# A two-layer trunk kernel: state-space channels projected first, rotation angles computed directly, array halves in turn

## The chip, the cores and the metric

One core of one Trainium2 chip runs the whole program. The metric is the device time of one execution in microseconds, taken as the median over executions of the same program; the profile is of one more execution.

## The reference

One inference step of a trunk of two layers for two request groups that share the weights. Cut to what matters here, layer 0:

```python
z = rmsnorm(x, g_mix[0]) @ w_in_mix        # columns: u (512) | q (512) | k (128) | v (128)
ya = s5_mixer(u, ...)                      # 32 groups of 16 channels, 64 complex states each:
                                           #   h_t = a h_{t-1} + b u_t,  y = Re(c h),  a = exp((lr + i li) dt)
yb = swa(q, k, v, rel_bias, sink)          # window of 128, 8 query heads on 2 key-value heads of 64
x = x + concat([ya, yb]) @ w_out_mix
x = x + conv_ffn(rmsnorm(x, g_ffn[0]))     # up-projection, causal convolution of width 3, gelu gate, down-projection
...
```

Layer 1 replaces the mixer by a convolution module and is not touched. Prompts have 1040 tokens (16 learned ones and 1024); 8 decoding requests add 8 tokens each with cached keys, values and states. Everything is float32 at the interface.

## The kernel before

The tokens are split into two streams that stay in SBUF with channels on partitions: **A** has 528 prompt tokens, **B** the other 512 prompt tokens and the 64 decoding ones (576). Every weight block goes through one path: DMA of a raw float32 tile, a rounded high part `whi` on ScalarE (L210), a low part `wlo` on VectorE (L216), and then for every 128 rows of the contraction three products with the high and low parts of the activations (L315), each over two halves of the stream's tokens. These are the `pu` rows of the trace: 264 columns for A, 288 for B, two matmuls each.

`run(items)` goes through a list of `Unit`s (one weight block on one stream; a `Pair` is two with one activation). After each of a Unit's contraction steps it calls `pump()`, which advances a list of background generators at their rates. The generators emit the work that isn't a projection: transposing the inputs (`take_x`, from L506), the tables of the state-space part (`s5_prep`, L823 to L879), its main loop (`s5_main`, L923 to L971), the attention of the prompts. An instruction's place in its engine's queue is the moment of emission, so the list of Units and the generators' `yield`s set the order on every engine; nothing is reordered afterwards. When the list asks for a result that a generator hasn't emitted, it pumps without Units until it has (`back()` waits so for the four parts of A's attention output, `atp`).

**Input projections.** `in_units` lists a stream's four u blocks, k, v and four q blocks. Before, A goes k and v as a Pair, q, then u; B goes u, then k, v, q. The epilogue of a u block is one VectorE operation of eight pieces (`us`, L1397), that of q and k one of 128x528 (`qst`, L530). `NU0` is how many u blocks must have been projected before `s5_main` starts; `nq`, counted by q's epilogue, releases A's attention.

**State-space part.** `s5_prep1` computes a = decay·(cos, sin) on VectorE and ScalarE. `s5_rot` makes the powers of the rotation by repeated squaring in small GpSimd operations (L709 to L726), combines them into tables ta and tb, and multiplies these into the four tables tj of 128x576 (L588 to L596) which go to DRAM. `table_e` and `table_f` build the tables ee (L823 to L828) and ff (L843 to L848) on VectorE, which PE transposes (psk L865, psf L879). `s5_main` runs eight iterations over four groups: stage 1 (L923) forms the chunk sums xr and xi, writing each half of the columns of the array; stage 2 scans on VectorE; stage 3 (L968 to L970) accumulates, for each half g2 and each gl, one product of 128 rows and two of 64 rows, twelve matmuls of 138 columns, in one PSUM bank per half.

**Prompt attention.** `attn_blocks` runs over tasks: for A one of 16 queries, one with 144 keys and three with 256 keys; for B four with 256 keys. A task is split by key-value head into two half-tasks of four query heads. A half-task computes scores (sps L1236, four matmuls of 64 rows in two emissions), adds the bias on VectorE (L1239), takes maxima (L1171), exponentials on ScalarE (L1178), normalizes (L1187), transposes the probabilities (tps L1218, evacuated by ScalarE L1220) and multiplies by v (ops L1256, 64 columns). Three half-tasks are in flight, with two buffers each for P, PT and q. A's attention runs at rate 1.6 beside the projections, B's at 0.7 beside the first up-projection of A.

## Time and profile before

| what | value |
|---|---|
| median of 3 runs | 2460.75 us (2455.71 to 2464.07) |
| profiled execution | 2459.83 us, of it 2457.7 us span |
| PE busy | 2386.9 us (97% of the span) |
| VectorE busy | 1695.9 us (69%) |
| ScalarE busy | 1001.6 us (41%) |
| GpSimd busy | 237.0 us (10%) |
| mean granted TensorE clock | 0.98 |
| chain that ended last | PE 86%, VectorE 6%, ScalarE 2%, DMA 1% |

The span runs from the first to the last instruction; the 2.1 us by which the execution is longer lie outside it. The chain goes back from the last instruction, at each step to what released it: four fifths of it are the projections of L315. A granted clock of 1.00 is the upper of TensorE's two levels, 2.4 GHz; a mean below that holds stretches at 1.2 GHz.

### The profile page before, as it was taken

The page shows a single profiled execution, that of the slowest core. Times are in us where ns is not written, and L with a number is a line of the kernel's source. Part 1 is how long each engine was busy: PE and PEld are TensorE (multiplying, and loading weights), DVE is VectorE, ACT ScalarE, POOL GpSimd, SP SyncE. Part 2 cuts the span into 40 slices and gives each one's busy share as a digit, 9 for nine tenths or more (in the row PEclk, how much of TensorE's full clock was granted, in tenths as well). Part 3 has the DMA queues.
Part 4 walks back from the last instruction along what each step waited for, and adds up shares of the span by engine and source line. Part 5 has one row for each costly group of instructions (what it writes and reads, how often), then busy time and mean ns, then how long its engine had stood idle before and what let it go on. Part 6 is the DMA issues. An engine that isn't in the chain of part 4 may idle for free.

```text
span 2457.7 us, 46157 instructions
## 1 busy us (share of the span) xinstructions
PE 2386.9 (97%) x18180; PEld 2313.4 (94%) x18180; DVE 1695.9 (69%) x3180; ACT 1001.6 (41%) x1912; POOL 237.0 (10%) x557
## 2 busy tenths in 40 slices
PE   7689999999999999999999999999999999999998
PEld 6677889888999999999999999999999999999998
DVE  6976657554477679888888567888889765444343
ACT  6133354664334343342426443443434534333333
POOL 5940120000000000110101000100000000000000
PEclk9889999999999999999999999999999999999999
DMA  7765753423333433222232432333232423222222
GB/s 211 222 128 134 223 147 118 111 68 95 97 93 89 137 100 97 82 82 85 80 89 70 129 125 74 101 92 95 86 98 80 130 74 114 80 87 79 86 85 70
DMA packets 459598, 260.86 MB, mean 106 GB/s; under 512 B 57451, under 2 KB 446727, under 8 KB 458198
## 3 DMA queue, kind: packets, MB, share of 16 engines
q1 hardware_dynamic: 456246, 253.08, 35.5%
q0 software_dynamic: 3136, 4.85, 0.8%
q8 instruction: 143, 2.34, 0.4%
q14 instruction: 73, 0.60, 0.1%
HBM read 225.59 MB, written 35.52 MB: 106 GB/s over the span
## 4 chain that ended last, share of the span: by engine, by line
PE 86%; DVE 6%; ACT 2%; DMA 1%; issue 1%; SPq 0%; POOL 0%; DVEq 0%; ACTq 0%
PE pu L315 80%; DVE wlo L216 1%; PE ops L1256 1%; PE sps L1236 1%; PE yps L969 1%; PE tps L1218 0%; PE yps L968 0%; ACT whi L210 0%; PE psum_s L367 0%; DMA xbD<-xB 0%; PE yps L970 0%; DMA e<-eD 0%; DVE xA L1187 0%; DVE mx L1171 0%; DVE us L1397 0%
## 5 line engine op out<-in xcount | busy, mean ns | idle before, releaser
L216 DVE TENSOR_TENSOR wlo<-raw,whi 128x512 fp32r<-128x512 f32 x720 | 489.8, 683 | 529.1 <-ACT whi L210 520.2
L210 ACT CAST whi<-raw 128x512 fp32r<-128x512 f32 x720 | 434.9, 608 | 695.1 <-PE pu L315 641.8
L1658 DVE SCALAR_TENSOR_TENSOR xA<-gl,pt,xA 128x528 f32<-128x528 f32 x240 | 183.2, 764 | 3.8 <-ACT xA L1652 1.5
L1658 DVE SCALAR_TENSOR_TENSOR xB<-gl,pt,xB 128x512 f32<-128x512 f32 x240 | 179.3, 747 | 4.3 <-ACT xB L1652 2.9
L1477 ACT ACTIVATE cv<-cv 128x592 f32<-128x592 f32 (+2 forms) x88 | 58.9, 670 | 154.5 <-DVE cv L1476 154.5
L1475 DVE SCALAR_TENSOR_TENSOR cv<-G,pt,cv 128x592 f32<-128x592 f32 (+2 forms) x88 | 70.1, 796 | 40.7 <-ACT cv L1474 40.0
L315 PE MATMUL pu<-a0h,whi 128*128 128x288 f32 (+3 forms) x428 | 91.5, 296 | 5.1 <-ACT a0h L212 1.9
L315 PE MATMUL pu<-a1h,whi 128*128 128x288 f32 (+3 forms) x428 | 92.0, 297 | 0.0
L315 PE MATMUL pu<-a4h,whi 128*128 128x288 f32 (+3 forms) x420 | 89.1, 294 | 2.6 <-ACT th L1405 2.5
L315 PE MATMUL pu<-a3h,whi 128*128 128x288 f32 (+3 forms) x428 | 91.1, 294 | 0.0
L315 PE MATMUL pu<-a2h,whi 128*128 128x288 f32 (+3 forms) x428 | 90.5, 293 | 0.0
L315 PE MATMUL pu<-a0l,whi 128*128 128x288 f32 (+3 forms) x428 | 90.1, 292 | 0.3 <-DVE a0l L218 0.3
L315 PE MATMUL pu<-a1h,wlo 128*128 128x288 f32 (+3 forms) x428 | 90.1, 293 | 0.0
L315 PE MATMUL pu<-a1l,whi 128*128 128x288 f32 (+3 forms) x428 | 90.0, 292 | 0.0
L315 PE MATMUL pu<-a0h,wlo 128*128 128x288 f32 (+3 forms) x428 | 89.8, 292 | 0.0
L315 PE MATMUL pu<-a7h,whi 128*128 128x288 f32 (+3 forms) x420 | 89.4, 295 | 0.0
L315 PE MATMUL pu<-a3h,wlo 128*128 128x288 f32 (+3 forms) x428 | 89.3, 290 | 0.0
L315 PE MATMUL pu<-a5h,whi 128*128 128x288 f32 (+3 forms) x420 | 89.1, 294 | 0.0
L315 PE MATMUL pu<-a2l,whi 128*128 128x288 f32 (+3 forms) x428 | 89.1, 290 | 0.0
L315 PE MATMUL pu<-a3l,whi 128*128 128x288 f32 (+3 forms) x428 | 89.0, 290 | 0.0
L315 PE MATMUL pu<-a6h,whi 128*128 128x288 f32 (+3 forms) x420 | 89.0, 294 | 0.0
L315 PE MATMUL pu<-a6l,whi 128*128 128x288 f32 (+3 forms) x420 | 88.0, 291 | 0.7 <-DVE a6l L216 0.7
(665 smaller groups left out, 6943.1 us busy)
## 6 DMA issues: line engine op xcount, KB each, us to landing
raw<-in_ffn_w_up SPq DMA_DIRECT2D x352, 256.0 KB, 2.9
raw<-in_ffn_w_down SPq DMA_DIRECT2D x128, 256.0 KB, 2.8
raw<-in_conv_w_pw SPq DMA_DIRECT2D x96, 256.0 KB, 2.8
raw<-in_ffn_w_down SPq DMA_DIRECT2D x64, 192.0 KB, 2.5
xbD<-xB SPq DMA_DIRECT2D x3, 2304.0 KB
xB<-xbD SPq DMA_DIRECT2D x6, 1152.0 KB
raw<-in_w_in_mix SPq DMA_DIRECT2D x24, 256.0 KB, 3.8
xaD<-xA SPq DMA_DIRECT2D x2, 2112.0 KB
```

The lines of the kernel that those rows point to most:

```text
L210: nc.scalar.copy(hi, src)
L216: nc.vector.tensor_tensor(lo, src, hi.bitcast(F32), op=OP.subtract)
L315: nc.tensor.matmul(ps[:, ch, :c], wt, xt[:, off + ch * c:off + (ch + 1) * c], start=(k == 0 and pi == 0), stop=(k == nk - 1 and pi == 2))
L969: nc.tensor.matmul(out, E[hs, 0, gl, :], H[hs, 0, gl, :], start=False, stop=False)
L1236: nc.tensor.matmul(v[:, hh, :], q[hs, 2 * pr + hh, :], self.kT[hs, kc0:kc0 + nk], start=True, stop=True)
L1256: nc.tensor.matmul(v, vt[:m, hs], d["PT"][k], start=(k == 0), stop=(k == len(vsegs) - 1))
L1475: nc.vector.scalar_tensor_tensor(c, G[:, 1:1 + n], wc(1), c, op0=OP.mult, op1=OP.add)
L1477: self.chain(lambda: None, lambda: None, lambda: nc.scalar.activation(c, c, AF.Gelu_apprx_tanh))
L1658: V.scalar_tensor_tensor(acc, gl[:, i:i + npp], w(i), acc, op0=OP.mult, op1=OP.add)
```

## The change

Five things are edited, all in layer 0's mixer.

1. The order of the input projections is now u of A, u of B, then k, v, q of A, then k, v, q of B; `NU0` falls from 8 to 6, and `nq` counts A's q blocks alone.
2. `s5_rot` computes the angles of ta and tb directly: the angle times a multiple, reduced by 2π in three parts, in fourteen GpSimd operations per table (16x16 and 16x9 columns), with the absolute value on VectorE and two sines on ScalarE. The tables tj come in halves with buffers of their own. The count of GpSimd's rows falls from 495 to 347.
3. Stage 3 takes both halves at once in two PSUM banks: four products of 128 rows, then eight of 64 rows that alternate between the upper and the lower half of the array's rows.
4. `attn_blocks` takes all eight heads as one task: scores alternate between the two halves of the rows (one per key-value head), outputs between the two halves of the columns, with one copy for both. P has one buffer, PT two; w1 and w2 are counts of `yield`s that spread a task.
5. `take_x` copies the second half of each of B's tiles on VectorE and not on ScalarE.

```diff
-NU0 = 8
+NU0 = 6
...
+                (nc.vector.tensor_copy if first or hf else nc.scalar.copy)(
                     x[:, 4 * hf:4 * hf + 4, lo:hi], f[:, :, lo - off:hi - off])
...
+        thh, thl = pl[:, 16, :], pl[:, 17, :]
+        V.tensor_scalar(thh, th, 12288.0, -12288.0, op0=OP.add, op1=OP.add)
+        V.tensor_tensor(thl, th, thh, op=OP.subtract)
...
     def s5_rot(self):
...
-        G.tensor_copy(e[:, 0, 0, :], cs)
-        G.tensor_copy(e[:, 0, 1, :], sn)
-        renorm(e[:, 0, 0, :], e[:, 0, 1, :])
-        for _ in range(3):
-            square(e[:, 0, 0, :], e[:, 0, 1, :], e[:, 0, 0, :], e[:, 0, 1, :])
-        for i in range(1, 8):
-            square(e[:, i, 0, :], e[:, i, 1, :], e[:, i - 1, 0, :], e[:, i - 1, 1, :])
...
+        for tt, mult in ((ta, self.mult[:, 0:16]), (tb, self.mult[:, 16:25])):
+            n = tt.shape[3]
+            v = lambda i: tz[:, 256 * i:256 * i + 16 * n].rearrange("p (g a) -> p g a", g=16)
+            x, k, w, h = (v(i) for i in range(4))
+            mb = mult.unsqueeze(1).to_broadcast([P, 16, n])
+            th = lambda i: self.pl[:, i, :].unsqueeze(2).to_broadcast([P, 16, n])
+            G.tensor_tensor(k, th(4), mb, op=OP.mult)
+            G.tensor_scalar(k, k, 1.0 / (2 * math.pi), MAGIC, op0=OP.mult, op1=OP.add)
+            G.tensor_scalar(k, k, MAGIC, None, op0=OP.subtract)
+            G.tensor_tensor(x, th(16), mb, op=OP.mult)
+            for c in TWOPI[:2]:
+                G.tensor_scalar(h, k, -c, None, op0=OP.mult)
+                G.tensor_tensor(x, x, h, op=OP.add)
+            G.tensor_tensor(w, th(17), mb, op=OP.mult)
+            G.tensor_scalar(h, k, -TWOPI[2], None, op0=OP.mult)
+            G.tensor_tensor(w, w, h, op=OP.add)
+            G.tensor_tensor(x, x, w, op=OP.add)
+            G.tensor_scalar(x, x, 3.1415925, -3.1415925, op0=OP.min, op1=OP.max)
+            nc.vector.scalar_tensor_tensor(h, x, -1.0, x, op0=OP.mult, op1=OP.max)
+            G.tensor_scalar(h, h, -1.0, math.pi / 2, op0=OP.mult, op1=OP.add)
+            nc.scalar.activation(tt[:, 0], h, AF.Sin)
+            nc.scalar.activation(tt[:, 1], x, AF.Sin)
         for j in range(4):
             g4 = slice(4 * j, 4 * j + 4)
-            tt = pp.tile([P, 2, 4, 9, 16], F32, name="tj", tag="tj")
             t1 = tz[:, 0:576].rearrange("p (g q b) -> p g q b", g=4, q=9)
             t2 = tz[:, 576:1152].rearrange("p (g q b) -> p g q b", g=4, q=9)
             f1 = lambda ri: ta[:, ri, g4, :].unsqueeze(2).to_broadcast([P, 4, 9, 16])
             f2 = lambda ri: tb[:, ri, g4, :].unsqueeze(3).to_broadcast([P, 4, 9, 16])
-            self.cmul(G, tt[:, 0], tt[:, 1], f1(0), f1(1), f2(0), f2(1), t1, t2)
             for ri in range(2):
-                nc.gpsimd.dma_start(self.dq(self.tD, ri, j, 132),
-                                    tt[:, ri].rearrange("p g q b -> p g (q b)")[:, :, 0:132])
+                G.tensor_tensor(t1, f1(0), f2(ri), op=OP.mult)
+                G.tensor_tensor(t2, f1(1), f2(1 - ri), op=OP.mult)
+                tt = pp.tile([P, 4, 9, 16], F32, name="tj", tag=f"tj{ri}")
+                G.tensor_tensor(tt, t1, t2, op=OP.add if ri else OP.subtract)
+                G.dma_start(self.dq(self.tD, ri, j, 132), tt.rearrange("p g q b -> p g (q b)")[:, :, 0:132])
...
-        def stage3(i, g2, ys):
+        def stage3(i, ys):
+
             u, m1, E, H = u_(i), m_(i), e_(i), h_(i)
-            ps = self.bank("yps")
-            hs = slice(64 * g2, 64 * g2 + 64)
+            mm = lambda out, w, x, start, stop: nc.tensor.matmul(out, w, x, start=start, stop=stop,
+                                                                 skip_group_check=True)
+            pss = [self.bank("yps"), self.bank("yps")]
+            out = lambda g2, gl: pss[g2][:, gl * NK:(gl + 1) * NK]
+            for g2 in range(2):
+                for gl in range(2):
+                    mm(out(g2, gl), m1[:, 2 * gl + g2, :], u[:, 2 * gl + g2, :], gl == 0, False)
             for gl in range(2):
-                out = ps[:, gl * NK:(gl + 1) * NK]
-                nc.tensor.matmul(out, m1[:, 2 * gl + g2, :], u[:, 2 * gl + g2, :], start=True, stop=False)
-                nc.tensor.matmul(out, E[hs, 0, gl, :], H[hs, 0, gl, :], start=False, stop=False)
-                nc.tensor.matmul(out, E[hs, 1, gl, :], H[hs, 1, gl, :], start=False, stop=True)
-            nc.scalar.copy(ys.rearrange("p (l h) k -> p l h k", h=2)[:, :, g2, :],
-                           ps[:, :2 * NK].rearrange("p (g k) -> p g k", g=2))
-            if g2:
-                for g in range(4):
-                    nc.gpsimd.dma_start(dap(self.yD, (4 * i + g) * 16 * 8 * NK, [[NK, 8], [8 * NK, 16], [1, NK]]),
-                                        ys[:, g, :])
+                for ri in range(2):
+                    for g2 in range(2):
+                        hs = slice(64 * g2, 64 * g2 + 64)
+                        mm(out(g2, gl), E[hs, ri, gl, :], H[hs, ri, gl, :], False, ri == 1)
+            for g2 in range(2):
+                nc.scalar.copy(ys.rearrange("p (l h) k -> p l h k", h=2)[:, :, g2, :],
+                               pss[g2][:, :2 * NK].rearrange("p (g k) -> p g k", g=2))
+            for g in range(4):
+                nc.gpsimd.dma_start(dap(self.yD, (4 * i + g) * 16 * 8 * NK, [[NK, 8], [8 * NK, 16], [1, NK]]),
+                                    ys[:, g, :])
...
-        self.atA = SB[:, 2048:2048 + 4 * 528].rearrange("p (j n) -> p j n", j=4)
-        v4 = lambda c, k: SA[:, c:c + 4 * k].rearrange("p (h k) -> p h k", h=4)
-        self.abuf = {"P": [v4(0, 256), v4(1024, 256)], "PT": [v4(2048, P), v4(2560, P)],
-                     "q": [v4(3072, P), v4(3584, P)]}
+        self.atA = SA[:, 2048:2048 + 4 * 528].rearrange("p (j n) -> p j n", j=4)
+        v8 = lambda t, c, k: t[:, c:c + 8 * k].rearrange("p (h k) -> p h k", h=8)
+        self.abuf = {"P": [v8(SA, 0, 256)], "PT": [v8(SB, 2048, P), v8(SB, 3072, P)],
+                     "q": [SB[:, 4096:4608].rearrange("p (h k) -> p h k", h=4)]}
...
         self.nbuf[kind] = self.nbuf.get(kind, 0) + 1
-        return self.abuf[kind][self.nbuf[kind] % 2]
...
-            self.nq += 1
+            self.nq += s is self.A
...
+        def turn(pt, task):
+            nq, out = task[1], []
+            for k, (vt, ko, m) in enumerate(task[5]):
+                t = self.buf("PT")[:m, :, :nq]
+                for kv in range(2):
+                    v = self.bank("tps").rearrange("p (h k) -> p h k", h=4)[:m, :, :nq]
+                    for h in range(4):
+                        nc.tensor.transpose(v[:, h, :], pt[:, 4 * kv + h, ko:ko + m], self.ident[:nq, :nq])
+                    nc.scalar.copy(t[:, 4 * kv:4 * kv + 4], v)
+                out.append(t)
+                yield out
+
+        def scores(i):
+            c0, nq, kc0, nk, bcol = tasks[i][:5]
+            q = qs[i]
+            pt = self.abuf["P"][0][:nq, :, :nk]
+            for pr in range(2):
+                vs = [self.bank("sps").rearrange("p (h k) -> p h k", h=2)[:nq, :, :nk] for _ in range(2)]
+                for hh in range(2):
+                    for kv, hs in enumerate(half):
+                        nc.tensor.matmul(vs[kv][:, hh, :], q[hs, 2 * pr + hh, :], self.kT[hs, kc0:kc0 + nk],
+                                         start=True, stop=True)
+                for kv in range(2):
+                    h0 = 4 * kv + 2 * pr
+                    V.scalar_tensor_tensor(pt[:, h0:h0 + 2, :], vs[kv], HD ** -0.5,
+                                           self.bias[:nq, h0:h0 + 2, bcol:bcol + nk], op0=OP.mult, op1=OP.add)
+                if pr == 0:
+                    yield pt
+
+        def output(task, pts):
+            c0, nq, kc0, nk, bcol, vsegs, oc = task
+            v = self.bank("ops").rearrange("p (h k) -> p h k", h=4)[:, :, :nq]
+            for k, (vt, ko, m) in enumerate(vsegs):
+                for kv, hs in enumerate(half):
+                    nc.tensor.matmul(v[hs], vt[:m, hs], pts[k][:, 4 * kv:4 * kv + 4, :],
+                                     start=(k == 0), stop=(k == len(vsegs) - 1))
+            nc.scalar.copy(at[:, :, oc:oc + nq], v)
...
+        n = len(tasks)
+        live = None
+        for i in range(n + 1):
+            if live:
+                pt, sm, es = live
+                self.softmax_fin(pt, 8, sm, es)
+                for _ in range(w2):
                     yield
-            if 0 <= i - 1 < n:
-                d = live[i - 1]
-                self.softmax_fin(d["P"], 4, *d["s"])
+                for pts in turn(pt, tasks[i - 1]):
+                    yield
+            if i < n:
+                for pt in scores(i):
+                    yield
+                live = (pt, *self.softmax_rows(pt, tasks[i][1], 8, tasks[i][3], self.sink, self.nsink))
+                load_q(i + 1)
+                yield
+            if i:
+                output(tasks[i - 1], pts)
                 yield
...
+                for _ in range(w1):
+                    yield
...
-        yield from self.attn_blocks(tasks, at)
+        yield from self.attn_blocks(tasks, at, 6, 3)
...
-        yield from self.attn_blocks(tasks, at)
+        yield from self.attn_blocks(tasks, at, 3, 2)
...
-        def in_units(s, h):
-            us = [Unit(self.wblock(win, 0, KT, j * P), h, s, self.epi_u(s, j)) for j in range(4)]
-            ks = [Unit(self.wblock(win, 0, KT, 1024), h, s, self.epi_k(s)),
-                  Unit(self.wblock(win, 0, KT, 1152), h, s, self.epi_v(s))]
-            return us, ks + [Unit(self.wblock_q(j), h, s, self.epi_q(s, j)) for j in range(4)]
-        uA, kA = in_units(A, lambda: self.hx["A"])
-        uB, kB = in_units(B, lambda: self.hx["B"])
-        items += [Pair(kA[0], kA[1])] + kA[2:] + uA + uB + kB
+        hA, hB = (lambda: self.hx["A"]), (lambda: self.hx["B"])
+        us = [[Unit(self.wblock(win, 0, KT, j * P), h, s, self.epi_u(s, j)) for j in range(4)]
+              for s, h in ((A, hA), (B, hB))]
+        items += [Pair(us[0][0], us[0][1])] + us[0][2:] + us[1]
+        for s, h in ((A, hA), (B, hB)):
+            items += [Unit(self.wblock(win, 0, KT, 1024), h, s, self.epi_k(s)),
+                      Unit(self.wblock(win, 0, KT, 1152), h, s, self.epi_v(s))]
+            items += [Unit(self.wblock_q(j), h, s, self.epi_q(s, j)) for j in range(4)]
```

The tail of A's prompt attention in PE's order (`sps` scores, `tps` transposes, `ops` outputs, `pu` projections; the last `pu` row ahead of the tail is the end of the input projections). Before:

```order
L1236 MATMUL sps<-kT,xA 128x256 x2
L315 MATMUL pu<-y5h,whi 128x288 x2
L315 MATMUL pu<-y5l,whi 128x288 x2
L315 MATMUL pu<-y5h,wlo 128x288 x2
L1256 MATMUL ops<-xA,vA 64x512 x2
L315 MATMUL pu<-y6h,whi 128x288 x2
L315 MATMUL pu<-y6l,whi 128x288 x2
L315 MATMUL pu<-y6h,wlo 128x288 x2
L1218 MATMUL tps<-ident,xA 128x128 x4
L315 MATMUL pu<-y7h,whi 128x288 x2
L315 MATMUL pu<-y7l,whi 128x288 x2
L315 MATMUL pu<-y7h,wlo 128x288 x2
```

and with the change:

```order
L321 MATMUL pu<-y7h,whi 128x288 x2
L321 MATMUL pu<-y7l,whi 128x288 x2
L321 MATMUL pu<-y7h,wlo 128x288 x2
L1232 MATMUL ops<-xB,vm 64x512 x2
L1232 MATMUL ops<-xB,vA 64x512 x2
L1205 MATMUL tps<-ident,xA 128x128 x16
L1218 MATMUL sps<-kT,xB 128x256 x8
L1232 MATMUL ops<-xB,vA 64x512 x4
L1205 MATMUL tps<-ident,xA 128x128 x16
L1218 MATMUL sps<-kT,xB 128x256 x8
L1232 MATMUL ops<-xB,vA 64x512 x4
L1205 MATMUL tps<-ident,xA 128x128 x16
L1232 MATMUL ops<-xB,vA 64x512 x4
```

Before, each emission of attention has three or more rows of projection behind it until the attention's end; now the last three tasks stand behind the last input projection with no projection between them.

The start on ScalarE, from the sine of the base angle (table load and `pl`), over the copies of the rope table (`Rk`), to the input transposes of B (squares into `junk`, copies of `xps`). Before:

```order
L673 ACT_TABLE_LOAD
L673 ACTIVATE pl<-pl 128x16
L674 ACTIVATE pl<-pl 128x16
L390 COPY Rk<-rps 128x512
L391 COPY Rk<-rps 128x16
L496 ACTIVATE junk,ssqB<-xrow 128x512
L508 COPY xB<-xps 128x4x128
L496 ACTIVATE junk,ssqB<-xrow 128x512
L508 COPY xB<-xps 128x4x128
```

and with the change:

```order
L678 ACT_TABLE_LOAD
L678 ACTIVATE pl<-pl 128x16
L679 ACTIVATE pl<-pl 128x16
L396 COPY Rk<-rps 128x512
L397 COPY Rk<-rps 128x16
L731 ACTIVATE ta<-tz 128x256
L732 ACTIVATE ta<-tz 128x256
L731 ACTIVATE tb<-tz 128x144
L732 ACTIVATE tb<-tz 128x144
L502 ACTIVATE junk,ssqB<-xrow 128x512
L514 COPY xB<-xps 128x4x128
```

Four sines of tables that GpSimd computes now stand ahead of the squares and copies of stream B.

## Rows read from the trace of the kernel before

**Rows 1.** Busy time by window: start:end, length; then each engine, clock, DMA share, GB/s.
```profile
30.00:122.00 92.00, 64.83 (x489) 59.44 (x488) 80.44 (x173) 36.35 (x87) 83.47 (x188) 0.87 0.72 218
122.00:389.00 267.00, 254.10 (x1681) 217.05 (x1679) 179.69 (x425) 108.11 (x273) 57.29 (x74) 0.94 0.58 152
440.00:600.00 160.00, 159.07 (x1140) 136.73 (x1139) 86.37 (x171) 91.49 (x190) 3.33 (x20) 1.00 0.28 81
```

**Rows 2.** PE's waits, 0 to 150 us: total us, times, longest.
```profile
PE psf L879 <- DVE ff L845: 10.9, 3, 5.0
PE vps L1159 <- ACT xB L508: 6.6, 1, 6.6
```

**Rows 3.** Timeline, GpSimd then ScalarE: start us, duration us; [idle before <-releaser].
```profile
30.51 0.19 POOL L725 COPY e<-pl 128x16 f32<-128x16 f32 x1 [21.31 <-ACT pl L674]
...
110.03 1.17 POOL L588 TENSOR_TENSOR tz<-ta,tb 128x576 f32<-128x576 f32 x1
111.16 1.94 POOL L589 TENSOR_TENSOR tz<-ta,tb 128x576 f32<-128x576 f32 x1
...
47.81 0.62 ACT L210 CAST whi<-raw 128x512 fp32r<-128x512 f32 x1 [5.78 <-DMA raw<-in_w_in_mix]
```

**Rows 4.** Timeline, VectorE, table work without and with GpSimd beside it.
```profile
71.19 1.04 DVE L843 TENSOR_TENSOR ff<-bb,apw 128x512 f32<-128x512 f32 x1
...
97.09 0.70 DVE L530 TENSOR_TENSOR qst<-pu,Rk 128x528 f32<-128x528 f32 x1
...
109.28 1.55 DVE L1397 TENSOR_TENSOR us<-pu,Rk 128x66 f32<-128x66 f32 x8
...
111.99 1.98 DVE L844 TENSOR_TENSOR y<-bb,apw 128x512 f32<-128x512 f32 x1
...
119.68 1.78 DVE L848 TENSOR_TENSOR ff<-ff,y 128x512 f32<-128x512 f32 x1
```

**Rows 5.** Timeline, PE, one state-space iteration: stage 1, then part of stage 3.
```profile
210.52 0.69 PE L923 MATMUL xr<-u,xf 128*64 128x138 f32 x8
211.04 0.64 PE L923 MATMUL xi<-u,xf 128*64 128x138 f32 x8
...
250.97 0.40 PE L968 MATMUL yps<-u,m 128*128 128x138 f32 x2
...
255.25 0.53 PE L315 MATMUL pu<-y1h,whi 128*128 128x288 f32 x2
```

**Rows 6.** Timeline, PE, prompt attention of A between projection rows.
```profile
176.74 1.13 PE L1236 MATMUL sps<-kT,xA 64*128 64x256 f32 x4
177.80 0.53 PE L315 MATMUL pu<-y3h,whi 128*128 128x288 f32 x2
178.17 0.42 PE L315 MATMUL pu<-y3l,whi 128*128 128x288 f32 x2
178.44 0.42 PE L315 MATMUL pu<-y3h,wlo 128*128 128x288 f32 x2
...
181.62 1.93 PE L1256 MATMUL ops<-xA,vA 128*64 128x512 f32 x4
183.48 0.53 PE L315 MATMUL pu<-y6h,whi 128*128 128x288 f32 x2
```

**Rows 7.** Groups of VectorE, then ScalarE, 440 to 600 us: busy us, mean ns.
```profile
L1239 DVE SCALAR_TENSOR_TENSOR P<-sps,bias 128x512 f32<-128x512 f32 x16 | 10.9, 686 | 2.8 <-PE sps L1236 2.8
L1171 DVE TENSOR_REDUCE mx<-P 128x4 f32<-128x1024 f32 x8 | 9.8, 1220 | 0.3
L1187 DVE TENSOR_SCALAR P<-P,smx 128x256 f32<-128x256 f32 x32 | 9.2, 350 | 0.3
...
L1178 ACT ACTIVATE P<-P,nm 128x256 f32<-128x256 f32 x32 | 15.9, 496 | 11.0 <-DVE nm L1173 10.8
L1220 ACT COPY PT<-tps 128x512 f32<-128x512 f32 x16 | 9.3, 585 | 5.7 <-PE tps L1218 5.3
L1178 ACT ACTIVATION_READ_ACCUMULATOR P<-P,nm 128x1 f32 x34 | 6.3, 187 | 0.0
```

**Rows 8.** Timeline, PE, first norm sums of stream A after the mixer.
```profile
388.61 1.17 PE L367 MATMUL psum_s<-ones,acc 128*128 128x1 f32 x10
```

More of the change, by code (lines that the diff above doesn't have):

```diff
@@ L60 @@
 Q2 = 5
+MAGIC = 12582912.0
+_C2 = math.floor((2 * math.pi - 6.28125) * 2 ** 21) / 2 ** 21
+TWOPI = (6.28125, _C2, 2 * math.pi - 6.28125 - _C2)
 class Stream:
@@ L98, with __init__ @@
 class Unit:
-    def __init__(self, w, act, s, epi, off=0, c=None):
+    def __init__(self, w, act, s, epi, off=0, c=None, hold=False):
         self.w = w
+        self.hold = hold
         self.act = act
@@ L316, in mm @@
                                          start=(k == 0 and pi == 0), stop=(k == nk - 1 and pi == 2))
-            for u in units if len(units) == 1 else ():
+            for u in units if len(units) == 1 and not units[0].hold else ():
                 for i, (k0, n) in enumerate(u.w.cuts):
@@ L507, in take_x @@
                 squares(2 * t + hf)
-                (nc.vector.tensor_copy if first else nc.scalar.copy)(
+                (nc.vector.tensor_copy if first or hf else nc.scalar.copy)(
                     x[:, 4 * hf:4 * hf + 4, lo:hi], f[:, :, lo - off:hi - off])
@@ L1187, in softmax_fin, with attn_blocks @@
             V.tensor_scalar(pt[:, h, :], pt[:, h, :], sm[:, h:h + 1], None, op0=OP.mult)
-    def attn_blocks(self, tasks, at):
+    def attn_blocks(self, tasks, at, w1, w2):
         nc = self.nc
         V = nc.vector
-        todo = [(t, kv) for t in tasks for kv in range(2)]
-        qs, live = {}, {}
+        qs = {}
+        half = [slice(0, 64), slice(64, 128)]
         def load_q(i):
```

119 lines of the change are left out of this document (19 added, 100 removed).

## The prediction

> **What bounds the kernel now.** I read the table of windows first [rows 1]. Between 30 and 122 us PE works 64.83 of 92 us while VectorE works 80.44 and GpSimd 83.47; the granted clock is 0.87 there. Between 122 and 389 us PE works 254.10 of 267 us at 0.94, and between 440 and 600 us, beside B's attention, 159.07 of 160 us at 1.00. So there are three regimes. In the first PE waits for others, and a shorter PE instruction is worth nothing. In the last a PE microsecond saved is a microsecond of the total. The second lies between: 12.9 us of idle time. The list of PE's waits [rows 2] says what it waits for at the start: 10.9 us for the table ff of VectorE, and once 6.6 us for ScalarE's copies of stream B. The first regime ends when ff's last operation ends on VectorE, at 119.68 + 1.78 = 121.46 us [rows 4]; the second at the first norm sums of A, 388.61 us [rows 8]. I price the change as a shift of these two points and of the stage behind.
>
> **First regime: the start, +23 us.** GpSimd gets its angle at 30.51 us [rows 3], as now. The sines of the first table need 13 of its operations of 256 columns, one absolute value on VectorE and one more operation; the second table the same at 144 columns. No row has these sizes. A 16-column operation lasts 0.19 us, a 576-column one 1.17 us [rows 3]; between them in proportion, 256 columns cost 0.6 us and 144 columns 0.4 us, together 14 x 0.6 + 14 x 0.4 = 14 us, and with the handovers and four sines ScalarE is past them near 47 us. Between ends far apart (28 operations at 0.19 give 36 us, at 1.17 give 63 us) I take the middle because the sizes lie there. ScalarE's queue holds the squares and copies of B behind the sines, 16.5 us late. VectorE has taken over some copies and gives perhaps 1.5 us back. The weight casts behind them waited 5.78 us for a DMA before, until 47.81 us [rows 3], and that wait absorbs the next 5 us: +10. PE's 6.6 us wait on these copies is inside, and grows.
>
> The u blocks of A now come first, so four epilogues of 1.55 us stand on VectorE where 0.70 us ones stood [rows 4]: +3.5.
>
> Then contention. Operations on table ff last 1.04 us with GpSimd on small operations, 1.98 us beside its 576-column ones [rows 4], which themselves go from 1.17 to 1.94 us [rows 3]. All 24 such GpSimd operations and their DMAs now start near 47 us and run some 40 us beside the tables; before only six ran there. If VectorE spends three quarters of 40 us on operations that lose 0.94 of every 1.98 us, that is 14 us, less the 5 us that the last table already paid: +9. The sum is +23. The ends: +6 with the sines past at 36 us and half the contention, +40 with them past at 63 us.
>
> The trace shows VectorE losing about 0.9 us per operation next to a GpSimd operation of 1.2 to 1.9 us, so less than one such operation. The Trainium skill, SBUF — State Buffer, section "Who interferes with whom", says that a VectorE instruction with two SBUF inputs and a GpSimd one that reads SBUF take the shared port for the whole instruction and the other blocks fully; by it the price could be all 24 operations.
>
> **Second regime: 121.5 to 388.6 us, -19 us.**
> - Stage 3: twelve matmuls take 255.25 - 250.97 = 4.28 us [rows 5], 0.36 each. Stage 1 shows what two halves in turn can give: eight records, which are four matmuls, in 211.04 - 210.52 = 0.52 us, 0.13 each [rows 5]. These are halves of the columns; for halves of the rows no row exists. I take half the time for the eight row-half matmuls: 4.28 to 2.8, eight times: -12. Bounds: 0 and -16 (at stage 1's rate).
> - Attention of A: scores of two heads take 177.80 - 176.74 = 1.06 us, outputs of a half-task 183.48 - 181.62 = 1.86 us [rows 6]. A task of 256 keys spends 4 x 1.06 + 2 x 1.86 = 8.0 us on them; in turn, half: -4.0. Three such tasks and about -2.5 for that of 144 keys: -14.5.
> - Switches: behind each emission the first projection row lasts 178.17 - 177.80 = 0.37 us where the next takes 0.27 [rows 6], and I estimate as much ahead of it: 0.2 us. Some 38 emissions fewer: -7.5.
> - State-space work starts after 6 u blocks and beside all of k, v and q, so its waits are better covered; of 12.9 us idle [rows 1] I take 11 away. The clock of 0.94 over 254 us costs some 15 us against 1.00; I take 9 of it back, since the next item makes a new hole.
> - **The tail: +35.** In the new order the last three tasks have no projection among them. One task then is a chain: four bias additions of 0.69 us and two maxima's worth of 1.22 us on VectorE, eight exponentials of 0.50 on ScalarE, eight scalings of 0.35, transposes with four copies of 0.59 [rows 7], partly overlapped, and outputs: 2.8 + 2.4 + 0.3 + 4.0 + 2.8 + 2.5 = 15 us. The first of the three has its scores just ahead of the end, so some 12 + 15 + 15 us, then 5 us for the last outputs, copies and splits: 47 us. PE's own work in it is about 12 us. Bounds: 25, if the chain overlaps better, and 50, if other work of VectorE and ScalarE stands in between.
>
> Together -12 - 14.5 - 7.5 - 11 - 9 + 35 = -19. Extra VectorE copies of `take_x` (item 5) are counted above; ScalarE's copy for both halves of the output replaces two, off PE's path here.
>
> **Third regime: -17 us.** B's attention has four tasks: -4.0 each is -16, and 40 emissions become 20, at 0.2 us: -4. PE had 0.9 us idle of 160 [rows 1], so it counts in full. P has a single buffer and all eight heads' softmax now come in one go; the projections between the emissions cover it, but I leave 3 us for waits. Everything after is unchanged.
>
> **Sum.** +23 - 19 - 17 = -13. The profiled execution took 2459.83 us (span 2457.7 and 2.1 around it), so 2446.8; the median of the runs is 0.9 higher. Forecast: **2448 us**, 0.5% faster.
>
> **Rivals.**
> 1. *The row halves don't overlap.* Everything shown to overlap is in halves of the columns [rows 5]; nothing in this trace shows it for rows. Then the scores save nothing (2.1 us per full task, seven tasks, and 1.2: 16 us) and stage 3 nothing (12 us): 2448 + 28 = 2476, slower. It decides if two paired score matmuls take over 0.8 of their serial time of 0.53 us each [rows 6]. Against it: the two halves go to different banks, so no output is shared.
> 2. *The lock is whole.* VectorE loses each GpSimd operation in full: 24 x 1.17 = 28 us, less 7 already paid, is +21 where I took +9: 2460, no change. For it: the price of 1.94 us on GpSimd's side [rows 3]; against it: 0.94 on VectorE's. The rule of the Trainium skill named above (SBUF — State Buffer, "Who interferes with whom") would have it so; the rows here agree with it in kind, not in size.
> 3. *The start is short.* GpSimd's operations stay near 0.25 us as its tiny ones and ScalarE is past the sines at 38 us; then the DMA wait hides the rest and the first regime gains only 8 us: 2433, faster.
> 4. *The head of the list changes little:* the tail is covered by whatever VectorE had pending and the front is DMA-bound either way: 2425.
>
> **How the numbers follow.** Chances: forecast 0.58, rival 1 0.12, rival 2 0.15, rival 3 0.10, rival 4 0.05. A measurement of this kernel tells about 0.3% from no change, 7.4 us: faster is below 2453.4, slower above 2468.1. The forecast's own bounds (front +6 to +40, tail 25 to 50) leave some 0.62 of it below, 0.28 between and 0.10 above. With rivals 3 and 4 faster, rival 1 slower, and rival 2 mostly between: faster 0.52, same 0.26, slower 0.22. The range reaches to rival 3 and rival 1: 2430 to 2478.
>
> **What would show it.** Right: in the new profile a PE idle stretch from near 34 to 50 us with ScalarE at the sines; ff's last operation near 145 us; stage 3 in under 3 us; scores of four heads in about 1.06 us; a stretch of some 47 us with PE a third busy before A's output projection; A's norm sums near 393 us; the stage from there to the end of B's attention some 17 us shorter. Wrong: if four score matmuls still take 2.1 us, or PE's idle time before 60 us stays below 10 us, or the tail is below 30 us.

## The result: 34 us slower, and the profile after

The changed kernel takes 2492.73 us (median of 4, 2490.73 to 2493.39) against 2458.23 us of before on the same chip: a ratio of 1.0136, 95% interval 1.0114 to 1.0157. Forecast were 2448 us and a range up to 2478; the time lies above it, on the other side of no change.

| | before | after |
|---|---|---|
| profiled execution, span | 2457.7 us | 2491.4 us |
| PE busy | 2386.9 us | 2348.2 us |
| mean granted clock | 0.980 | 0.966 |
| last transposes of ff begin | 121.6 us | 154.0 us |
| first norm sums of A | 388.61 us | 428.88 us |

PE works 38.7 us less and the kernel ends 33.7 us later, so 72 us of idle time on PE came in. To see where, I set the two PE timelines side by side by their projections: the time at which the n-th record of a projection (`pu`) begins, counted over the whole timeline.

```
n-th pu record       50    200    350    650    960   1040   1700   2600   3200
before             27.8   68.8  105.4  191.9  290.5  318.5  412.8  558.9  656.6
after              29.6  105.8  142.5  206.6  284.4  363.7  452.9  600.1  691.2
after - before     +1.8  +37.0  +37.1  +14.8   -6.1  +45.2  +40.1  +41.1  +34.6
```

The 960th record ends the input projections. Four stretches: the start loses 37 us; the stretch of state-space loop and attention up to the last input projection wins 43; a hole behind it loses 51; the rest gives back 11. The table of windows of the changed kernel (columns as in [rows 1]) shows the first three, the start in three rows:

```profile
30.00:60.00 30.00, 14.45 (x83) 13.26 (x81) 15.40 (x55) 12.14 (x35) 24.96 (x36) 0.67 0.52 161
60.00:90.00 30.00, 16.44 (x83) 15.01 (x84) 29.71 (x38) 5.27 (x14) 27.59 (x24) 0.61 0.59 109
90.00:155.00 65.00, 46.59 (x333) 42.67 (x333) 63.40 (x143) 17.60 (x39) 0.00 (x0) 0.82 0.79 225
155.00:286.00 131.00, 119.50 (x985) 108.44 (x986) 83.41 (x228) 50.61 (x141) 28.27 (x49) 0.93 0.74 193
286.00:349.00 63.00, 25.12 (x110) 15.89 (x106) 24.00 (x54) 36.48 (x83) 0.00 (x0) 0.67 0.13 32
```

At the start PE is busy 14.45 of 30 us, then 16.44 of 30, where [rows 1] had 64.83 of 92; then 119.50 of 131; and between 286 and 349 us 25.12 of 63 us at a clock of 0.67. PE's waits name the causes (columns as in [rows 2]); first up to 125 us, then from 286 to 410 us:

```profile
PE pu L321 <- DVE us L1399: 13.3, 3, 7.2
PE bps L1072 <- DVE xA L1064: 9.7, 1, 9.7
PE xps L512 <- DVE xB L514: 9.2, 1, 9.2
```

```profile
PE tps L1205 <- DVE xA L1178: 30.6, 3, 11.8
```

PE waits for the epilogues `us` of the u blocks, for a small memset of the attention's set-up (`xA`, L1064) and a copy of B, which stand in VectorE's queue, and then, in the hole, for VectorE's softmax (`xA`, L1178).

**The start.** The timeline of ScalarE (start, duration) shows it standing before the sines of the two tables:

```profile
41.80 0.42 ACT L731 ACTIVATE ta<-tz 128x256 f32<-128x256 f32 x1 [9.13 <-POOL tz L730]
...
49.44 0.32 ACT L731 ACTIVATE tb<-tz 128x144 f32<-128x144 f32 x1 [6.92 <-POOL tz L730]
...
49.88 0.61 ACT L502 ACTIVATE junk<-xrow 128x512 f32<-128x512 f32 x1
```

The squares of B begin at 49.88 us, which was 30.88 us before. VectorE's timeline shows a wait for GpSimd of similar length, and then something I had priced too low, ordinary small operations that last as long as GpSimd's:

```profile
48.70 0.31 DVE L729 SCALAR_TENSOR_TENSOR tz<-tz 128x144 f32<-128x144 f32 x1 [7.42 <-POOL tz L728]
...
65.12 9.65 DVE L222 TENSOR_TENSOR wlo<-raw,whi 128x512 fp32r<-128x512 f32 x4
...
79.50 3.04 DVE L602 TENSOR_TENSOR apw<-tw,tv 128x32 f32<-128x32 f32 x1
```

Four `wlo` take 9.65 us (0.69 each when alone), an operation of 128x32 takes 3.04 us (0.18 alone). GpSimd's multiplications aren't slowed meanwhile:

```profile
80.20 1.17 POOL L740 TENSOR_TENSOR tz<-ta,tb 128x576 f32<-128x576 f32 x1
```

Every third operation of GpSimd, which adds or subtracts, lasts 1.40 to 1.75 us, and 1.43 to 1.44 in one_tj below.

**The halves.** They do what they were meant to do (PE timeline): the scores of 256 keys, then stage 3 of one iteration.

```profile
280.52 1.13 PE L1218 MATMUL sps<-kT,xB 64*128 64x256 f32 x8
281.58 0.54 PE L321 MATMUL pu<-y6h,whi 128*128 128x288 f32 x2
```

```profile
214.61 1.10 PE L951 MATMUL yps<-u,m 128*128 128x138 f32 x8
215.64 1.21 PE L951 MATMUL yps<-H,e 64*128 64x138 f32 x16
216.78 0.53 PE L321 MATMUL pu<-y5h,whi 128*128 128x288 f32 x2
```

Four score matmuls in 281.58 - 280.52 = 1.06 us, the time of two in [rows 6]; twelve matmuls of stage 3 in 216.78 - 214.61 = 2.17 us, 4.28 in [rows 5].

**The tail.** From the last input projection to A's output projection nothing but attention is left on PE:

```profile
294.46 3.87 PE L1205 MATMUL tps<-ident,xA 128*128 128x128 f32 x16 [7.76 <-DVE xA L1178]
304.23 4.26 PE L1218 MATMUL sps<-kT,xB 64*128 64x256 f32 x16 [5.89 <-ACT xB L1206]
...
321.38 3.93 PE L1205 MATMUL tps<-ident,xA 128*128 128x128 f32 x16 [11.02 <-DVE xA L1178]
...
341.03 3.93 PE L1205 MATMUL tps<-ident,xA 128*128 128x128 f32 x16 [11.83 <-DVE xA L1178]
344.88 2.44 PE L1232 MATMUL ops<-xB,vA 128*64 128x512 f32 x8
348.70 0.51 PE L321 MATMUL pu<-a4h,whi 128*128 128x264 f32 x2 [1.38 <-ACT a4h L216]
```

From the end of the row before it (`pu<-y7h,wlo`, 284.27 + 0.42) to 348.70 us are 64.0 us, where 47 were forecast. ScalarE shows what the chain has besides the exponentials: the gelu of stream B's state-space output, with its table load and once a wait for a DMA. Behind the first softmax it stands ahead of the copies of the transposes, for which the next scores wait:

```profile
300.46 1.28 ACT L1048 ACT_TABLE_LOAD   x1 [7.76 <-DMA yrd<-yD]
301.76 1.23 ACT L1048 ACTIVATE gt<-yrd 128x576 f32<-128x576 f32 x1
303.02 0.67 ACT L216 CAST y4h<-gt 128x576 fp32r<-128x576 f32 x1
303.60 2.04 ACT L1206 COPY xB<-tps 128x512 f32<-128x512 f32 x4
```

Behind the two later ones it goes by VectorE's queue: the low part of the gelu's result (`y7l`) stands ahead of the scalings that finish the softmax (`xA`, L1178), and waits for the gelu's cast:

```profile
338.71 0.67 ACT L216 CAST y7h<-gt 128x576 fp32r<-128x576 f32 x1
339.42 0.76 DVE L222 TENSOR_TENSOR y7l<-gt,y7h 128x576 fp32r<-128x576 f32 x1 [7.72 <-ACT y7h L216]
340.53 2.19 DVE L1178 TENSOR_SCALAR xA<-xA,smx 128x256 f32<-128x256 f32 x8
```

The transposes of 341.03 us follow. In the chain that ended last, this gelu work and the DMA ahead of it take some 17 of the 64 us.

### The profile page after: what moved, and what is told of

Read it like the earlier page. It is cut to its first block, busy times and chain, and to the rows that moved or that the text cites. A ratio compares the mean times of both kernels' runs of the same rounds, so it can differ in the third digit from the quotient of the medians.

```text
span 2491.4 us, 45976 instructions
## 1 busy us (share of the span) xinstructions
PE 2348.2 (94%) x18180; PEld 2297.1 (92%) x18180; DVE 1693.7 (68%) x3144; ACT 999.4 (40%) x1898; POOL 174.4 (7%) x405
## 4 chain that ended last, share of the span: by engine, by line
PE 78%; DVE 5%; ACT 3%; DMA 1%; issue 1%; SPq 0%; ACTq 0%; DVEq 0%
PE pu L321 75%; DVE wlo L222 1%; PE tps L1205 1%; DVE mx L1162 1%; ACT P L1169 1%; ACT xA L1169 1%; PE sps L1218 1%; ACT whi L216 0%; PE psum_s L373 0%; DMA xbD<-xB 0%; DMA fstt<-in_state_ffn 0%; DMA yrd<-yD 0%; DVE P L1222 0%; DMA xA<-xaD 0%; DMA raw<-in_ffn_w_up 0%
## 5 line engine op out<-in xcount | busy, mean ns | idle before, releaser
L321 PE MATMUL pu<-a2h,wlo 128*128 128x288 f32 (+3 forms) x428 | 88.9, 289 | 0.0
```

The lines of the kernel that those rows point to most:

```text
L321: nc.tensor.matmul(ps[:, ch, :c], wt, xt[:, off + ch * c:off + (ch + 1) * c], start=(k == 0 and pi == 0), stop=(k == nk - 1 and pi == 2))
```

## Experiments

My theory after this: the new order of projections exposes the tail; the direct angles cost the start, by held queues (VectorE and ScalarE wait for the sines) and by GpSimd's multiplications beside VectorE; the halves in turn gain. The rivals: the u blocks themselves make the start late, or the eight-head tasks make the tail. All ratios are to the kernel before on the same chip; "us" behind them is the ratio less 1, times 2456. Each run has one profile; in six that share the old order and the old angles the last ff transposes begin between 118.7 and 121.6 us five times and once at 127.3, so a difference of several us at the start can be chance.

### Which part of the change costs: halves_only, old_rot, old_order

**halves_only** undoes the order and the angles, **old_rot** the angles alone, **old_order** the order alone:

```diff
-        items += [Pair(us[0][0], us[0][1])] + us[0][2:] + us[1]
...
+        items += [Pair(kA[0], kA[1])] + kA[2:] + uA + uB + kB
...
-NU0 = 6
+NU0 = 8
...
-        for tt, mult in ((ta, self.mult[:, 0:16]), (tb, self.mult[:, 16:25])):
...
+            square(e[:, i, 0, :], e[:, i, 1, :], e[:, i - 1, 0, :], e[:, i - 1, 1, :])
```

> The changed kernel with the old order of projections (state-space start at 8 u blocks) and the old rotation by squaring; the array halves in turn stay. Theory (rotation costs the start 30 to 37 us, the new order exposes the prompt attention's tail at some 50 us, the halves gain): 2458 - 17 (stage 3) - 13 (attention of A) - 6 (attention of B) = 2422, between 2415 and 2435. Rival (eight heads in one task expose the tail whatever the order): 2465 or more. Rival (row halves gain nothing in the total): 2455 to 2460.

> The changed kernel with the old rotation by squaring, new order kept. Theory (the direct angles hold ScalarE and VectorE at the start and their GpSimd work then slows VectorE): the last ff transposes fall from 154.6 us to 125 to 130, total 2493 - 28 = 2465, between 2455 and 2475. Rival (the start is late because u blocks come first, with longer epilogues): the total stays above 2485.

> The changed kernel with the old order of projections and 8 u blocks before the state-space loop; direct angles and halves kept. Theory: the start stays late (last ff transposes at 150 us or later), the exposed tail of some 60 us goes, total 2422 + 33 = 2455, between 2445 and 2468. Rival (the tail belongs to the eight-head tasks): total above 2480 and a stretch of 40 us or more without projections before A's output projection.

| ratio (95% interval) | old angles | direct angles |
|---|---|---|
| old order | halves_only 0.9915 (0.9890 to 0.9939), -21 us | old_order 0.9998 (0.9984 to 1.0012), 0 us |
| new order | old_rot 1.0138 (1.0116 to 1.0159), +34 us | after 1.0136 (1.0114 to 1.0157), +33 us |

Two of three came as expected; old_rot came out in its rival's range, though its start was not late as the rival had it. The order costs 55 us with the old angles and 34 with the direct ones, and with both PE's timeline shows the tail: in old_rot the last outputs of A's attention begin at 339.08 us, in after at 344.88, in halves_only at 245.94. old_order has no such tail with its eight-head tasks, and its last ff transposes begin at 153.2 us although its u blocks come late: so the eight heads alone don't make the tail, nor the u blocks the late start. The angles cost 20 us in the old order. In the new one they cost nothing, which I had not expected. The start of old_rot is early as forecast (last ff transposes at 126.52 us, against 154.0), but PE's waits from 130 us on have a new one:

```profile
PE tps L1224 <- DVE xA L1197: 34.6, 4, 11.8
PE xr L928 <- DMA xf<-xfD: 21.4, 2, 14.4
```

The queue of SyncE, its timeline and then its longest wait between 120 and 165 us, shows what the loop waits for:

```profile
157.78 0.55 SPq L916 DMA_DIRECT2D T<-tD  x1
...
159.02 0.52 SPq L916 DMA_DIRECT2D xf<-xfD  x1
```

```profile
SPq L916 <- POOL tz L598: 17.2, 1, 17.2
```

The load of the rotation table T stands in the queue until 157.78 us, 17.2 us of it waiting for GpSimd, which is still multiplying out the table, and the second xf load stands behind it. So in this order the loop has to wait for the old rotation by squaring, and the 27 us gained at the start are lost there: the first stage 3 begins at 182.4 us, against 182.0 in after. GpSimd itself waits 9.5 us between 124 and 157 us for the stores of its tables, which have one buffer in the old rotation; what two buffers would give was not run.

### Why the start is late: one_tj, no_block, and both

**one_tj** multiplies out one of four table groups (the output's rotations are those of the first group), **no_block** takes the absolute values off VectorE and emits the sines ten pumps later:

```diff
+                if j == 0:
                     G.tensor_tensor(t1, f1(0), f2(ri), op=OP.mult)
...
-            nc.vector.scalar_tensor_tensor(h, x, -1.0, x, op0=OP.mult, op1=OP.max)
...
+        for _ in range(10):
+            yield
+        for tt, x in xs:
+            nc.scalar.activation(tt[:, 0], x, AF.Abs)
+            nc.scalar.activation(tt[:, 0], tt[:, 0], AF.Sin, scale=-1.0, bias=hp)
+            nc.scalar.activation(tt[:, 1], x, AF.Sin)
```

> The changed kernel, but only the first of the four table groups tj is multiplied out (6 of 24 GpSimd operations of 576 columns); its two halves are stored in all four places, so three quarters of the rotation table hold the first quarter's values. Theory (GpSimd's multiplications hold VectorE from 50 to 90 us): VectorE's four wlo at 65 us take under 3 us in place of 9.65 us, last ff transposes 15 to 22 us earlier than 154.6, total 2473 (2465 to 2482). Rival (only the wait for the sines costs): under 5 us earlier, total 2488 to 2494.

> The changed kernel with the angles on GpSimd as they are, but VectorE's absolute values moved to ScalarE and the four sines emitted ten pumps later, behind most of stream B's squares, copies and casts; GpSimd's 24 multiplications stay. Theory (half of the late start is the queues of VectorE and ScalarE held for the sines, the other half GpSimd's multiplications beside VectorE): PE idle time between 30 and 60 us falls from 15 us to under 6, last ff transposes from 154 us to 138 (130 to 146), total 2493 - 12 = 2481 (2472 to 2487). Rival (the multiplications alone): last ff transposes at 150 us or later, total 2487 or more. Rival (the held queues alone): 130 us or earlier and 2470 or less.

> no_block and one_tj together: sines behind stream B's copies and only the first table group multiplied out (three quarters of the rotation table hold the first quarter's values). Theory (the held queues and the multiplications cover each other, so that each alone gave some 8 us and both give the whole late start): last ff transposes at 125 to 132 us as in old_rot, and no wait for the DMA of xf as there, total 2493 - 27 = 2466 (2458 to 2474). Rival (a third cause in the new order, the u blocks ahead): last ff transposes at 138 us or later, total 2476 or more.

| | ratio | last ff transposes begin |
|---|---|---|
| after | 1.0136 (1.0114 to 1.0157) | 154.0 us |
| one_tj | 1.0138 (1.0118 to 1.0157) | 146.9 us |
| no_block | 1.0112 (1.0080 to 1.0143) | 146.4 us |
| both | 1.0051 (1.0032 to 1.0070) | 132.9 us |

At the last ff transposes each alone gives 7 to 8 us, both together 21: the two causes cover one another. (Two more profiles with the start of after, old_attn and glu_first below, have 153.2 us.) In the total neither alone is clear of the intervals, and both together are. Against 121.6 us before, 11 us remain, which no run takes apart. one_tj's total missed (2488.40 us against 2473; its rival had 2488 to 2494, but with the transposes under 5 us earlier), although VectorE did what was expected:

```profile
61.80 2.51 DVE L222 TENSOR_TENSOR wlo<-raw,whi 128x512 fp32r<-128x512 f32 x4
...
67.59 0.23 DVE L602 TENSOR_TENSOR apw<-tw,tv 128x64 f32<-128x64 f32 x1
81.50 0.69 DVE L222 TENSOR_TENSOR wlo<-raw,whi 128x512 fp32r<-128x512 f32 x1 [13.69 <-ACT whi L216]
```

Four `wlo` take 2.51 us where they took 9.65, and the work from the first power table (56.95 us in after, 55.93 here) to the last (L602 at 64 columns) ends at 67.82 and not at 88.95 us: the 18 of GpSimd's 24 operations that one_tj leaves out cost VectorE 32.0 - 11.9 = 20 us, 1.1 us each. But then VectorE waits 13.69 us for a weight. SyncE's waits say why:

```profile
SPq L1403 <- DVE us L1402: 25.5, 2, 24.6
```

The stores of u stand in SyncE's queue ahead of the next weights and waited 25.5 us for the epilogues `us`, which stand on VectorE behind the absolute values and B's copies; in after the longest of these waits is 26.6 us. The loads then come in one go: between 70 and 80 us no engine computes, and the DMA share is 1.11. So what the sines hold is not only VectorE and ScalarE but, through the u store, the weight loads. In no_block the longest wait for `us` falls to 10.2 us, but the longest for VectorE's `wlo` grows from 12.8 to 19.2, which fits multiplications that run beside more of VectorE's work: PE works 20.51 of 30 us between 30 and 60 us (9.5 us idle, under 6 expected), but 10.04 of 30 between 60 and 90. Its total came as expected (2480.16 us), its ff transposes later than the 130 to 146 us. The expectations for the single runs took the two as a sum; for both together 2466 us were expected and 2466.72 measured, with the transposes at 132.9 us (125 to 132 expected).

### Why the tail is long: old_attn, glu_first

**old_attn** puts the half-tasks of before into the changed kernel, **glu_first** moves work into the tail:

```diff
-        add(back)
-        items += oA[:OA] + gluA + oA[OA:] + [lambda: self.reload(B)] + [lambda: self.banks(3)] + yaAu
+        items += gluA
+        add(back)
+        items += oA + [lambda: self.reload(B)] + [lambda: self.banks(3)] + yaAu
```

> The changed kernel with the attention of before (half-tasks of four heads, three in flight, no turns); order of projections, angles and stage 3 as changed. Theory (the order exposes the tail, whatever the tasks): 40 us or more between the last input projection and A's output projection, total 2485 to 2510, since the gain of the turns is lost as well. Rival (eight heads with a single P buffer make the tail): tail under 40 us, total 2480 or less.

> The changed kernel with the four units of A's gate (48 projection rows, some 13 us) in the list ahead of A's attention output, so that they stand between the scores and transposes of the tail. Theory (PE only lacks other work in the tail): 2493 - 11 = 2482 (2477 to 2487). Rival (the tail is bound by ScalarE, which also has the gelu of these units): 2488 or more.

old_attn: 1.0168 (1.0136 to 1.0199), as expected. The tail stays, so the order makes it. From the last input projection (295.75 + 0.42 us) to A's output projection it lasts 47.9 us and not 64.0:

```profile
295.75 0.42 PE L321 MATMUL pu<-y7h,wlo 128*128 128x288 f32 x2
...
305.50 1.18 PE L1227 MATMUL sps<-kT,xA 64*128 64x256 f32 x4 [2.99 <-ACT xB L1248]
...
344.05 0.51 PE L321 MATMUL pu<-a4h,whi 128*128 128x264 f32 x2 [1.33 <-ACT a4h L216]
```

Here PE waits 3 us at a time for copies and not 11 for a softmax: three half-tasks overlap, while a task of eight heads with a single P buffer has its stages one after another. That the single P buffer is the reason is argued: buffers, heads and turns change together here. The longer tail of the eight heads costs 16 us; what their turns save on PE ahead of it (the 960th projection record at 284.4 us in after, 295.9 in old_attn) pays for most of it. glu_first: 1.0127 (1.0109 to 1.0146), 2484.70 us; A's norm sums begin at 421.3 us against 428.9. These 7.6 us are below the 11 that the theory expects, and in the ratio the gain is 2 us and within the intervals, so the run decides little.

### What the halves are worth: serial_halves, halves_noB, split_softmax, split_b, halves_nu6

All five start from halves_only. **serial_halves** has the same matmuls in another order; **halves_noB** gives B the attention of before; **split_softmax** and **split_b** emit the softmax in two batches of four heads, everywhere or for B alone; **halves_nu6** has `NU0` at 6.

```diff
-                for hh in range(2):
-                    for kv, hs in enumerate(half):
+                for kv, hs in enumerate(half):
+                    for hh in range(2):
...
-                live = (pt, *self.softmax_rows(pt, tasks[i][1], 8, tasks[i][3], self.sink, self.nsink))
+                for kv in range(2):
+                    live.append(self.softmax_rows(pt[:, sl], tasks[i][1], 4, tasks[i][3], self.sink[:, sl],
...
-NU0 = 8
+NU0 = 6
```

> As halves_only, but with the same matmuls in another order: scores first both of the upper rows, then both of the lower; in stage 3 the four 64-row products of one half, then those of the other. Theory (only neighbours on different row halves overlap): the four score matmuls take 1.5 to 2.1 us in place of 1.06, stage 3 about 3 us in place of 2.2, total 2433 + 10 = 2443 (2438 to 2452). Rival (the gain is in the batches and not in the turns, or PE's time there is covered anyway): under 2437.

> As halves_only, but B's attention as before (half-tasks of four heads, three in flight, no turns); A's attention and stage 3 in turn. Theory (B's stage gives back half of what it saves: about 20 us of PE time saved, 8 gained): 2433 + 8 = 2441 (2436 to 2447). Rival 1 (B gains in full): 2448 or more. Rival 2 (B gains nothing): 2429 to 2436.

> As halves_only (old order, old rotation, halves in turn), but the softmax of a task is emitted in two batches of four heads with yields between them. Theory (in B's stage the eight exponentials in one go hold ScalarE and with it the evacuation G, on which PE waits 5.0 us in halves_only and then runs some rows at the lower clock): that wait goes, total 2433 - 6 = 2427 (2420 to 2432). Rival (the wait is made up elsewhere): 2432 to 2440.

> As halves_only, with the softmax in two batches of four heads in B's attention alone (A's stays as in halves_only; two yields fewer between tasks so that B's attention keeps its length). Theory (the eight exponentials in one go keep ScalarE from the evacuation G, on which PE waits 5.0 us in halves_only): no wait for G above 1 us, PE idle time in B's stage under 3 us, total 2433 - 5 = 2428 (2423 to 2431). Rival (the wait moves to the gate product cv of VectorE, as it did when A's attention was split as well): idle time of 5 us or more, total 2432 or more.

> As halves_only, but the state-space loop may start after 6 u blocks, 48 projection rows earlier. Theory (nothing waits for the loop's end in the old order): 2433, within 5 us. Rival (the early start lets projections cover the loop's waits): 2428 or less.

| run | ratio (95% interval) |
|---|---|
| halves_only | 0.9915 (0.9890 to 0.9939) |
| serial_halves | 0.9909 (0.9876 to 0.9942) |
| halves_noB | 0.9942 (0.9924 to 0.9960) |
| split_softmax | 0.9974 (0.9956 to 0.9992) |
| split_b | 0.9910 (0.9878 to 0.9941) |
| halves_nu6 | 0.9980 (0.9966 to 0.9994) |

serial_halves missed, and the number of its rival holds: the total is the same. Its scores last as long as in turn, and only the eight products of stage 3 are longer (1.71 us to the next row, 1.14 in after):

```profile
165.30 1.14 PE L1237 MATMUL sps<-kT,xB 64*128 64x256 f32 x8
166.37 0.53 PE L321 MATMUL pu<-y0h,whi 128*128 128x288 f32 x2
...
241.71 1.78 PE L970 MATMUL yps<-H,e 64*128 64x138 f32 x16
243.42 0.53 PE L321 MATMUL pu<-y7h,whi 128*128 128x288 f32 x2
```

Two scores on the upper rows followed by two on the lower overlap as fully as four in turn. The single records of that stage 3 show how far: the second half's first record begins at 242.28 us, with the fifth of the first half's eight, and the last four stand alone again. So it isn't the turns but having both halves in one emission that gains (what the two banks do in it was not tested); the remaining 0.57 us in eight iterations are too little to be seen in the total.

halves_noB: B's halves are worth 0.0027, some 7 us as expected, though the intervals overlap. PE's busy time rises by 2351.8 - 2338.2 = 13.6 us without them, so half of it was given back. In halves_only's B stage PE waits once for 5.0 us for ScalarE, whose eight exponentials and their table load stand from 430.66 to 436 us ahead of the copy G; with the old half-tasks its longest wait there is 0.8 us, and with two batches (split_b) the one long wait becomes several (PE's waits, from 415 us on for the first two, from 360 us on for split_b):

```profile
PE pu L321 <- ACT G L1477: 5.0, 1, 5.0
PE pu L321 <- DVE cv L1509: 2.1, 3, 1.5
```

```profile
PE tps L1310 <- DVE P L1197: 0.8, 1, 0.8
```

```profile
PE tps L1306 <- DVE P L1197: 4.1, 5, 2.3
PE pu L321 <- DVE cv L1598: 3.0, 1, 3.0
PE pu L321 <- ACT G L1566: 1.8, 1, 1.8
```

The rival of split_b holds: the wait moves, 8.9 us in seven waits for 7.1 in four, the total is the same. split_softmax and halves_nu6 both lose, 0.0059 and 0.0065 against halves_only, which neither their theories nor their rivals had. In halves_nu6 the loop starts earlier beside A's attention, and the stretch between the 650th and the 725th projection record takes 211.0 - 172.2 = 38.8 us where halves_only has 189.1 - 171.6 = 17.5; some of that is loop work that comes earlier, since 15 us remain at the 1700th record and at the end. In split_softmax only 8 of the profile's 21 us stand at the 3200th record and the rest behind it, so why it loses stays open.

halves_only is the version to keep: it beats both kernels, 0.9915 of before and 0.978 of the changed one (0.9915 / 1.0136). It keeps the copies of `take_x` on VectorE (item 5 of the change), which no run takes apart.

## Why the prediction was wrong

Three steps of the sum failed, all by their size: the contention of GpSimd and VectorE at the start (+9 forecast), the chain of the tail (47 us forecast, 64.0 measured) and, for B's attention, "it counts in full". The four terms, each measured by the projection records above (start: the 350th; loop and attention without the tail: to the 960th, and the last row's stretch between the 1040th and the 1700th; tail: the 960th to the 1040th; B: behind the 1700th):

| term | forecast | measured |
|---|---|---|
| start | +23 | +37 |
| loop and A's attention, without the tail | -54 | -43 - 5 = -48 |
| tail | +35 | +51 |
| B's attention and after | -17 | -6 |
| sum | -13 | +34 |

The records don't part the loop and the tail cleanly: before, the last three of the eight stage 3 and one stage 1, 16 us, still stood behind the 960th record, and now they stand ahead of it.

- **The start** was mis-sized in its contention step. The sines came at 49.4 us (47 forecast), the squares 19 us late (16.5). But "VectorE spends three quarters of 40 us on operations that lose 0.94 of every 1.98 us: +9" took the price from a stretch where GpSimd, too, was slowed. The run one_tj measured 20 us for 18 of the 24 operations. That is rival 2, the whole lock, at +21: GpSimd's multiplications keep their 1.17 us, VectorE's 0.18 us operation lasts 3.04, the length of two of GpSimd's and more. The rule of the Trainium skill that the prediction names (SBUF — State Buffer, "Who interferes with whom") is the better description of this stretch. Missing altogether was SyncE's queue, where the store of u holds back the weights.
- **The loop and A's attention** were right within 6 us in sum, with other shares: stage 3 gave 2.1 us per iteration (1.5 forecast), 17 us in eight, more than the bound of 16, since the four products of 128 rows in a batch also went from 0.36 to 0.26 us each. That the sum came close is partly luck: the waits and the clock that were to give back 11 and 9 us did not, as PE is idle 11.5 of 131 us between 155 and 286 us, at 0.93. Rival 1 (no overlap of the rows) was wrong.
- **The tail** was the right mechanism at the wrong size: 64.0 us where 47 were forecast. "12 + 15 + 15 us, then 5" happens to be what the half-tasks take (47.9 us in old_attn); I had put eight heads into one chain without adding what else stands in it: per task the gelu's table load (1.28 us), a gelu, its cast and its low part on VectorE, 4 us in all, and once some 6 us for a DMA. Together that is some 17 us of the chain, as much as the forecast was short. The table load for the exponentials is not among them; it falls into a wait of ScalarE.
- **B's stage**: "it counts in full" was the failed step. By halves_noB 13.6 us of PE time went, where 20 were forecast, and the eight exponentials in one go brought a wait of 5.0 us (4.9 in the changed kernel). Around and behind it, from 420 to 460 us of halves_only, the granted clock is 0.90 and 0.93, where halves_noB has 1.00 throughout (windows of the two runs, columns as in [rows 1]):

```profile
420.00:440.00 20.00, 15.03 (x114) 14.31 (x113) 11.28 (x17) 11.36 (x27) 0.33 (x2) 0.90 0.26 75
440.00:460.00 20.00, 20.00 (x137) 16.58 (x136) 13.94 (x27) 10.43 (x20) 0.24 (x2) 0.93 0.30 87
```

```profile
420.00:440.00 20.00, 19.16 (x138) 17.11 (x137) 12.27 (x24) 13.07 (x28) 0.22 (x2) 1.00 0.23 67
```

All four errors had the same sign, and their sum, 47 us, is what separates -13 from +34. The range took the bounds of one or two of them at a time, and reached to rival 1, the wrong one.

## What to carry to other kernels

When a change shortens an instruction on the engine that is 97% busy, look first at what the new order puts into the gap: here 39 us of PE work went and 72 us of idle time came. A chain that was spread between projections is not free when it stands alone; add up every instruction of the engines it crosses, other work in their queues and table loads too. And two causes that stand over the same wait don't add: take both away before judging either.

## What the runs showed of the hardware that was not expected

- VectorE beside 576-column GpSimd operations: single operations of 0.18 us lasted 2.9 to 3.0 us, four of 0.69 us 9.65 us, while GpSimd's multiplications stayed at 1.16 to 1.19 us. In the kernel before, operations of VectorE lost 0.9 us and GpSimd's grew to 1.94 [rows 3, 4].
- Products of 64 rows in the two halves of the rows overlap even when they don't alternate: two and two take 1.06 us as in turn; four and four take 1.71 us against 1.14 in turn. In the records of four and four the second half starts when two products of the first, four of its eight records, have begun; two and two is then all overlap, as measured. No run tests other counts.
- Four products of 128 rows in a batch began 0.26 us apart, where the twelve products of stage 3 before, of 128 and 64 rows, began 0.36 us apart on average [rows 5].
